# The bonus and the output gate of a delta-rule scan formed in the projections' stage instead of per unit of the scan

## The chip, the cores and the metric

The kernel runs on one core of a Trainium2 chip. A core has a matrix engine (TensorE, in the profile PE, its weight loads PEld), a vector engine (VectorE, DVE), a scalar engine (ScalarE, ACT), a general one (GpSimd, POOL) and a queue from which DMA transfers are issued (SyncE, SP). The metric is the time of one execution on the device in microseconds, less being better; the time of a kernel is the median of three runs.

## The reference

Two layers over 1024 tokens of width 1024, all in float32. The first has a convolution and a gated unit as its mixer, the second RWKV-7 time mixing; each is followed by a feed-forward block. The change touches the time mixing alone, whose last lines matter here:

```python
w_log = -softplus(-(w0 + tanh(xw @ w_w1) @ w_w2)) - 0.5      # low-rank map, inner width 64
a = sigmoid(a0 + (xa @ a_w1) @ a_w2)                         # low-rank map, inner width 64
g = sigmoid(xg @ g_w1) @ g_w2                                # the gate, inner width 128
...
# per token: state <- state * w + (state . -kk) (kk * a)^T + v k^T ;  y = state . r
y = groupnorm(y) * ln_g + ln_b
bonus = sum(r * k * r_k, over the 64 channels of a head) * v
y = y + bonus
return (y * g) @ w_out
```

There are 16 heads of 64 channels. `r`, `k` and `v` are products of a shifted mixture of the tokens with three 1024x1024 matrices.

## The kernel before

**Stages.** In order: the convolution mixer, the first feed-forward block, the projections (`phase_c`), the scan (`phase_d`), the output projection of the time mixing (`phase_e`), the second feed-forward block.

**Precision.** Products of large matrices are made of three (`mm3`, `proj_T`, `proj_tok`): weights and activations are split into a high and a low part, and high x high, low x high and high x low are summed. `load_unit` loads a piece of 128x1024 weights and splits it, the high part on ScalarE (`whi`), the low one on VectorE (`wlo`). The scan's small products are in float32 or float16.

**Projections.** `phase_c` goes through two halves of 512 tokens: `do_r(0)`, `do_k(0)`, `do_v(0)`, `do_k(1)`, `do_r(1)`, `do_v(1)`. Between their large products, light jobs are woven in by `step`: the two low-rank maps (`light` and `lora2`, with tiles `pl`; the inner width of 64 is stored as 64 high and 64 low columns, `whl`), the inner half of the gate (`ghid`), and the mixing of tokens. The results `r`, `k`, the normalised `k` and so on go to DRAM tensors (`scr_R`, `scr_K`, ..., `scr_v`), one transfer per 128x512 block, issued from SP's queue.

**Scan.** The recurrence is done by chunks of 64 tokens, 16 chunks and two groups of eight heads: 32 units. A unit is a set of generators, each of which does one step when it is called: `load` and `load_v` fetch its data; `cumulate` (E) and `decay` (D) form the running decays; `scores` (P) forms the products within the chunk (`pA`), masks them (`ra`, the lower triangle copied to `lt`), the bonus (`pb`), the keys' transposes (`ptm`) and the triangle's transposes (`pL`); `inverse` (I) inverts the triangle in five doublings of two steps (`pX`, `pQ`, with copies by ScalarE and VectorE); `chain` (C) makes the products with the state: `pz`, its copy `zr`, `p`, `py`, `pS`, the normalisation (`gve`, `grs`) and the gate (`pg`, copied to `gg`); `store` (Y) writes the result.

**Order.** One iteration of the scan's loop advances unit i in C, unit i+1 in I, unit i+2 in P and later ones in D and E. The string `ORDER` says in which order their steps are emitted. Only the first matmul of a step is fixed against its neighbours (`keep` with `pace`); the framework's scheduler may move the rest within an engine's queue. After each step of C, I or P the loop yields; the first 32 such turns (`SCAN_EARLY`) run inside `do_v(1)`, between its products `pv`, the others inside `phase_e`, which weaves the loads of its own weights (`w_o`) and the first pieces of its work between them.

**The pieces in question.** Per unit, the bonus takes on POOL a product of `r` and `k`, on TensorE eight products of one column (`pb`), on VectorE a copy (`bon`). The gate takes two products of 64x256 (`pg<-g,ghid`) in float32 from `ghid`, which stays in SBUF, and a copy by ScalarE.

Of the kernel before, what the change touches and what calls it, by code (L numbers as in the profile page):

```python
# [25 lines left out]
P = 128  # L26
# [32 lines left out]
def f(ap):  # L59
    return ap.bitcast(F32)  # L60
# [16 lines left out]
ORDER = "ICIPCEIPDICPIECDICPIYCICPDICI"  # L77
# [12 lines left out]
def build(tc, xT, xtok, w_ab, w_abv, w_abo, cols, rows, hrows, sguw, f_in, f_out, w_r, w_k, w_v, w_o,  # L90
          l_w1, l_a1, l_g1, l_w2, l_a2, l_g2, out, dbg=None):
    nc = tc.nc
    c = Ctx()
    c.tc, c.nc = tc, nc
    c.first_loads = None
    with ExitStack() as es:
        setup(c, es, rows, hrows)
        dram = es.enter_context(tc.tile_pool(name="dram", bufs=1, space=DRAM))
        xres = dram.tile([T, D], F32, name="xres")
        scr = {n: dram.tile([8, P, 8, P], F32, name=f"scr_{n}") for n in ("R", "K", "KN", "KA", "SW")}  # L100
        scrv = dram.tile([T, D], F32, name="scr_v")
        scry = dram.tile([T, D], F32, name="scr_y")

        def show(n, tiles):
# [11 lines left out]
        scan = phase_d(c, scr, scrv, scry, l_g2)  # L116
        phase_c(c, x1, scr, scrv, w_r, w_k, w_v, l_w1, l_a1, l_g1, l_w2, l_a2, scan)
# [711 lines left out]
def phase_c(c, x1, scr, scrv, w_r, w_k, w_v, l_w1, l_a1, l_g1, l_w2, l_a2, scan):  # L829
    nc = c.nc  # L830
    sel2 = c.scan.sel2
    ghid = c.ghid = big(c, "ghid")
# [49 lines left out]
    def light(h, i, src, m, func, out):  # L882
# [6 lines left out]
        def steps():  # L889
# [25 lines left out]
            if not pair:  # L915
                nc.scalar.activation(out, p, func)
                return
# [8 lines left out]
            split(c, out[0][0:m], out[1], t_)  # L926
            if pair:
                nc.vector.tensor_copy(out[0][m:], f(out[0][0:m]))
# [10 lines left out]
    def lora2(u, hid, k):  # L939
        p = bank(c, "c", "pl")  # L940
        s = slice(k * P, (k + 1) * P)
        nc.tensor.matmul(p, u[:, s], hid[0], start=True, stop=False)
        c.last_mm = nc.tensor.matmul(p, u[0:64, s], hid[1], start=False, stop=True)
        return p

    def low_rank(h):

        hid = []
        for n in range(2):
            t_ = c.pool.tile([P, 1024], F32R, name="hid", tag="row", bufs=2)  # L950
            hid.append((t_[:, 0:512], t_[0:64, 512:1024]))
# [15 lines left out]
    def gate(h):  # L967
        light(h, 5, l_g1, P, AF.Sigmoid, ghid[:, h * TH:(h + 1) * TH])
# [79 lines left out]

    sp = Ring(c, "sp", 512, 4)
# [9 lines left out]
    xk = heavy(1, 2)  # L1059
    do_v(0, xv, rest)  # L1060
# [18 lines left out]
def scan_const(c):  # L1079
# [8 lines left out]
                            channel_multiplier=-1)  # L1088
    s.ident16 = const.tile([P, P], F16, name="ident16")
# [58 lines left out]
def phase_d(c, scr, scrv, scry, l_g2):  # L1148
# [19 lines left out]
    ghid, R1 = c.ghid, {}  # L1168
# [9 lines left out]
    rings([("R", 3), ("cl", 2), ("Em", 2), ("rk", 2), ("S", 2 * NG), ("dS", 2), ("u1", 2), ("y", 3),  # L1178
           ("V", 4), ("gg", 2), ("bo", 2)], W)
# [11 lines left out]
    for b in R1["G"].bufs + R1["lt"].bufs + [f(b) for b in R1["TT"].bufs]:  # L1191
        nc.gpsimd.memset(b, 0.0)
    S = [None] * NG
# [34 lines left out]
    def load_v(u):  # L1228

        src = scrv[u.ch * CH:(u.ch + 1) * CH, u.g * 2 * W:(u.g + 1) * 2 * W].rearrange(  # L1230
            "t (k e j) -> t e k j", k=HP, e=2)
        u.UV = R1["UV"]().rearrange("p (e k j) -> p e k j", e=2, k=HP)
        u.V = A4(R1["V"]())
        for e in range(2):
            nc.sync.dma_start(u.UV[half[e], e], src[:, e])
            nc.sync.dma_start(u.V[half[e]], src[:, e])
# [21 lines left out]
    def decay(u):  # L1258
# [6 lines left out]
        u.bk, u.rk = A4(R1["bk"]()), A4(R1["rk"]())  # L1265
# [6 lines left out]
        for e in range(2):  # L1272
            nc.gpsimd.tensor_tensor(u.rk[half[e]], ld["R"][half[e]], u.xk[half[e], :, e, :], op=ALU.mult)
        yield

    def scores(u):
# [31 lines left out]
        yield  # L1308
# [6 lines left out]
        nc.vector.copy_predicated(level_view(u.Tm, 1, False), sc.mT[1].unsqueeze(3), level_view(u.L, 1, False))  # L1315
# [33 lines left out]
    def chain(u, nxt):  # L1349
# [73 lines left out]
        nc.gpsimd.tensor_tensor(bo, u.V, bc(u.bon), op=ALU.mult)  # L1423
        nc.gpsimd.tensor_tensor(y, y, bo, op=ALU.add)
        yield
        pg = A4(bank(c, "c", "pg")[:, 0:W])
        for e in range(2):
# [35 lines left out]
    for i in range(-INV - 1, len(seq)):  # L1463
# [15 lines left out]
        if i > 0:  # L1479
            gens["Y"] = store(us[i - 1])  # L1480
        if i == 0:
            g2 = c.pool.tile([P, 1024], F32, name="g2", tag="w", bufs=N_W)
            nc.sync.dma_start(g2, l_g2)
            g2 = g2.rearrange("p (g k e j) -> p g e k j", g=NG, k=HP, e=2)
# [185 lines left out]
```

## Time and profile before

| | us |
|---|---|
| median of three runs | 2592.91 (2592.89 to 2593.0) |
| the profiled execution, its time | 2591.67 |
| its span, first to last instruction | 2590.0 |
| projections up to the last value projection, 1026.0 to 1343.0 | 317.0 |
| last value projection with the scan's first turns, 1343.0 to 1397.0 | 54.0 |
| scan, units 4 to 10 | 97.2 |
| scan, units 11 to 27 | 208.3 |

The profile was taken of one execution. "Busy" is the time in which an engine works on an instruction; x is a number of instructions; PEclk is the share of full speed that TensorE's clock was granted, with two levels, 1.2 and 2.4 GHz. A row of the timeline has the start in us, the duration in us, the engine, the line of the kernel, the operation, what is written and read, the shape, and in brackets the time that the engine sat idle before and what ended it. Units of the scan are counted from 0, from one `gve` to the next.

### The profile page before, as it was taken

What the parts mean: (1) busy time and instruction counts of PE and PEld (TensorE: products, weight loads), DVE (VectorE), ACT (ScalarE), POOL (GpSimd) and SP (SyncE); (2) the same over time, 40 slices, a digit from 0 to 9 for tenths busy, and PEclk for the clock granted to TensorE, in tenths of its full rate; (3) what the DMA queues carried; (4) which work ended last, traced back from release to release, by engine and by line L of the source; (5) the groups of instructions that cost most, each with busy time, mean ns of one, the idle gap of its engine ahead of it and who ended that gap; (6) DMA issues with size and microseconds to landing.
All of it is one profiled execution on the core that took longest, in us unless ns stands there. A gap on an engine that the chain in (4) does not pass through costs nothing.

```text
span 2590.0 us, 41379 instructions
## 1 busy us (share of the span) xinstructions
PE 2487.4 (96%) x16064; PEld 1981.5 (77%) x16064; DVE 1703.2 (66%) x2981; ACT 1135.7 (44%) x2192; POOL 519.0 (20%) x526
## 2 busy tenths in 40 slices
PE   8999989999999999999999888889999999999997
PEld 6677867888878787677777777777877888878785
DVE  7766596665657545878775778875676666657444
ACT  3115553333322334868655767774452233232230
POOL 0011250000006000010112666666300000006004
PEclk9999999999999999999999989999999999999998
DMA  4403222222225452555575444423412222225441
GB/s 149 128 9 122 90 98 96 83 74 85 85 95 195 140 177 90 155 143 174 166 195 142 101 102 105 88 59 101 155 66 98 82 82 81 82 101 197 156 157 65
DMA packets 257605, 295.79 MB, mean 114 GB/s; under 512 B 149888, under 2 KB 190976, under 8 KB 257408
## 3 DMA queue, kind: packets, MB, share of 16 engines
q1 hardware_dynamic: 256256, 291.05, 36.2%
q8 instruction: 126, 2.06, 0.3%
q10 hardware_dynamic: 1152, 2.10, 0.2%
q14 instruction: 71, 0.58, 0.1%
HBM read 219.56 MB, written 69.21 MB: 111 GB/s over the span
## 4 chain that ended last, share of the span: by engine, by line
PE 68%; DVE 10%; issue 9%; ACT 5%; DMA 5%; POOL 3%; SPq 0%; DVEq 0%; ACTq 0%; POOLq 0%
PE py L646 14%; PE pz L646 9%; PE px L646 8%; PE po L232 2%; DMA wraw<-in_f_out_dram 2%; PE po L233 2%; PE po L234 2%; PE pd L232 2%; PE pd L233 2%; PE pd L234 2%; PE pv L232 2%; PE pX L1204 1%; PE pv L233 1%; PE pA L1204 1%; PE pv L234 1%
## 5 line engine op out<-in xcount | busy, mean ns | idle before, releaser
L646 PE MATMUL py<-xch,wb 128*128 128x512 f32 x1056 | 355.7, 399 | 3.2 <-DVE u L695 2.8
L200 ACT CAST wb<-wraw 128x512 fp32r<-128x512 f32 x220 | 135.6, 620 | 394.3 <-PE py L646 177.9
L232 PE MATMUL pd<-wb,hh 128*128 128x512 f32 x704 | 277.1, 394 | 3.4 <-DVE acc L735 3.3
L234 PE MATMUL pd<-wb,hl 128*128 128x512 f32 x704 | 277.2, 394 | 0.0
L233 PE MATMUL pd<-wb,hh 128*128 128x512 f32 x704 | 276.8, 393 | 0.0
L646 PEld LDWEIGHTS py<-xch,wb 128*128 128x128 f32 x1056 | 199.6, 189 | 61.9 <-DVE u L695 16.0
L355 POOL TENSOR_TENSOR acc<-acc,g_row 128x1024 f32<-128x1024 f32 x24 | 67.4, 2807 | 889.9 <-DMA acc<-res 882.4
L203 DVE TENSOR_TENSOR wb<-wraw,wb 128x512 fp32r<-128x512 f32 x220 | 171.4, 783 | 103.6 <-ACT wb L200 101.2
L646 PE MATMUL px<-xch,wb 128*128 128x512 f32 x704 | 234.5, 396 | 3.2 <-ACT p L657 3.2
L646 PE MATMUL pz<-xch,wb 128*128 128x512 f32 x704 | 233.0, 392 | 4.5 <-ACT xch L200 4.5
L200 ACT CAST wb<-sums 128x512 fp32r<-128x512 f32 x176 | 108.9, 621 | 257.5 <-PE pz L646 144.6
L646 PE MATMUL py<-xcl,wb 128*128 128x512 f32 x528 | 208.6, 395 | 1.1 <-DVE xcl L203 0.9
L203 DVE TENSOR_TENSOR wb<-sums,wb 128x512 fp32r<-128x512 f32 x176 | 123.2, 703 | 107.0 <-ACT wb L200 106.1
L203 DVE TENSOR_TENSOR hl<-wraw,hh 128x1024 fp32r<-128x1024 f32 x72 | 124.2, 1734 | 87.8 <-ACT hh L200 87.7
L232 PEld LDWEIGHTS pd<-wb,hh 128*128 128x128 f32 x704 | 132.7, 189 | 35.5 <-DVE acc L735 4.5
L646 PEld LDWEIGHTS px<-xch,wb 128*128 128x128 f32 x704 | 132.9, 189 | 35.0 <-ACT p L657 4.7
L646 PEld LDWEIGHTS pz<-xch,wb 128*128 128x128 f32 x704 | 132.2, 188 | 34.4 <-ACT xch L200 5.3
L233 PEld LDWEIGHTS pd<-wb,hh 128*128 128x128 f32 x704 | 132.4, 188 | 29.6
L234 PEld LDWEIGHTS pd<-wb,hl 128*128 128x128 f32 x704 | 132.3, 188 | 29.4
L193 DVE TENSOR_TENSOR wlo<-wraw,whi 128x1024 fp32r<-128x1024 f32 x82 | 105.1, 1289 | 60.0 <-ACT whi L192 36.3
L1204 PEld LDWEIGHTS <-lt 128*128 128x128 f16 x1792 | 84.1, 99 | 73.9 <-issue 49.1
L646 PE MATMUL px<-xcl,wb 128*128 128x512 f32 x352 | 139.5, 396 | 0.0
(313 smaller groups left out, 5615.1 us busy)
## 6 DMA issues: line engine op xcount, KB each, us to landing
wraw<-in_f_in_dram SPq DMA_DIRECT2D x96, 512.0 KB, 3.6
wraw<-scr_h SPq DMA_DIRECT2D x72, 512.0 KB, 3.6
scr_h<-hf SPq DMA_DIRECT2D x44, 512.0 KB, 2.6
wraw<-in_f_out_dram SPq DMA_DIRECT2D x88, 256.0 KB, 2.8
res<-acc SPq DMA_DIRECT2D x16, 512.0 KB, 2.6
acc<-res SPq DMA_DIRECT2D x16, 512.0 KB, 4.2
wraw<-in_w_r_dram SPq DMA_DIRECT2D x16, 512.0 KB, 4.1
wraw<-in_w_k_dram SPq DMA_DIRECT2D x16, 512.0 KB, 4.2
```

The source lines that it names most:

```text
L193: (lo_eng or nc.vector).tensor_tensor(lo, raw, f(hi), op=ALU.subtract)
L200: nc.scalar.copy(hi, src)
L203: return (eng or nc.vector).tensor_tensor(lo, src, f(hi), op=ALU.subtract)
L232: nc.tensor.matmul(ps, ls(ah), rs(bh), start=start, stop=False)
L233: nc.tensor.matmul(ps, ls(ah), rs(bl), start=False, stop=False)
L234: c.last_mm = nc.tensor.matmul(ps, ls(al), rs(bh), start=False, stop=stop)
L355: c.nc.gpsimd.tensor_tensor(x, x, rows[0], op=ALU.mult)
L646: c.last_mm = nc.tensor.matmul(ps, a_[:, k * P:(k + 1) * P], b_[:, k % 2, :], start=start and k == i == 0, stop=False, skip_group_check=True)
L1204: keep(nc.tensor.matmul(*a, **k))
```

## The change

The gate is formed in `phase_c`: `ghid` is split into a high and a low part, and `gates(h)` makes for each half of the tokens eight tiles of 128x512 by three products each, copies them and stores them to a DRAM tensor `scr_g`. The bonus's sums are formed there too: `bonus(h)` loads the blocks of `r` and `k` back, multiplies them on POOL and sums over channels by products with `rkb`, a matrix of 128x2 that holds `r_k` for the two heads of a block (`pbn`), and stores them to `scr_b`. In the scan, a unit loads its gate (two transfers more, 15 instead of 13 per unit) and finds the sums in `bon`. The products `pb` and `pg`, POOL's product and two copies are gone from the unit. `scores` makes the triangle's transposes as its third step and the keys' as its fourth; before it was the keys' in its fourth and the triangle's in its fifth. The low-rank products with the low half use full 128x128 weights, where one operand was 64 columns (L903) or 64 rows (L943) before.

```diff
-ORDER = "ICIPCEIPDICPIECDICPIYCICPDICI"
+ORDER = "ICIPCEIPDICCIECDIPIYCIPDICI"
...
-                    nc.tensor.matmul(p[0:m, :], u[:, k, 0, :], r[k // 2][1][:, k % 2, 0:TH],
+                    nc.tensor.matmul(p, u[:, k].rearrange("p e m -> p (e m)"), r[k // 2][1][:, k % 2, 0:TH],
...
-        c.last_mm = nc.tensor.matmul(p, u[0:64, s], hid[1], start=False, stop=True)
+        c.last_mm = nc.tensor.matmul(p, u[:, s], hid[1], start=False, stop=True)
...
+    def gates(h):
+        g2 = load_unit(c, l_g2)
+        for t in range(4 * h, 4 * h + 4):
+            for n in range(2):
+                p = bank(c, "b", "pg")
+                mm3(c, p, ghid, g2, True, True, lambda g: g[:, t * P:(t + 1) * P], lambda w: w[:, n * 512:(n + 1) * 512])
+                gg = tmp(c, "gg")
+                nc.scalar.copy(gg, p)
+                nc.sync.dma_start(scrg[t * P:(t + 1) * P, n * 512:(n + 1) * 512], gg)
+                if (t, n) != (4 * h + 3, 1):
+                    yield
...
+    def bonus(h):
+        out = c.pool.tile([P, 4, 2, 8], F32, name="bons", tag="bons", bufs=1)
+        rk = None
+        for k in range(KT + 1):
+            if k:
+                p = bank(c, "b", "pbn", [P, 4, 2])
+                for t in range(4):
+                    nc.tensor.matmul(p[:, t, :], rk[:, t * P:(t + 1) * P], c.scan.rkb[:, k - 1, :], start=True, stop=True)
+                nc.vector.tensor_copy(out[:, :, :, k - 1], p)
+            if k < KT:
+                pair = []
+                for n in "RK":
+                    t_ = tmp(c, "rk")
+                    nc.sync.dma_start(t_.rearrange("p (c t) -> p c t", c=4),
+                                      scr[n][4 * h:4 * h + 4, :, k, :].rearrange("c p t -> p c t"))
+                    pair.append(t_)
+                rk = pair[0]
+                nc.gpsimd.tensor_tensor(rk, rk, pair[1], op=ALU.mult)
+                yield
...
+    add(gates(0), KT)
+    add(bonus(0), KT + 1)
     do_v(0, xv, rest)
...
+    add(gates(1), KT)
     do_r(1, xr, rest)
 
+    add(bonus(1), KT + 1)
     turns = itertools.islice(scan, SCAN_EARLY)
     do_v(1, xv, turn=lambda k: k % 2 and next(turns, None))
...
+            nc.sync.dma_start(u.gg[half[e]], src[1][:, e])
...
-        pb = bank(c, "c", "pb")
-        for k, e in PAIRS:
-            mm(pb[half[e], k:k + 1], u.rk[half[e], k, :], c.colr("r_k", u.g * HP + k, 1)[half[e]],
-               start=True, stop=True)
-        u.bon = small(c, [P, HP], "bon", "bon", NA)
-        nc.vector.tensor_copy(u.bon, pb[:, 0:HP])
-        yield
...
-        pg = A4(bank(c, "c", "pg")[:, 0:W])
-        for e in range(2):
-            mm(pg[half[e]], ghid[:, ch * CH:(ch + 1) * CH], g2[:, g, e], start=True, stop=True)
-        gg = A4(R1["gg"]())
-        nc.scalar.copy(gg, pg)
-        nc.gpsimd.tensor_tensor(y, y, gg, op=ALU.mult)
+        nc.gpsimd.tensor_tensor(y, y, u.gg, op=ALU.mult)
```

The scan's program moves at three places. The first is TensorE's queue in the last value projection, where `pv` are the value products and `pX`, `pQ` belong to the inverse of the first unit. Before:

```order
L234 MATMUL pv<-whi,xil 128x512
L1204 LDWEIGHTS lt
L1204 MATMUL pX<-lt 128x64
...
L1204 LDWEIGHTS lt
L1204 MATMUL pQ<-lt 128x64
...
L232 MATMUL pv<-whi,xih 128x512
L233 MATMUL pv<-wlo,xih 128x512
L234 MATMUL pv<-whi,xil 128x512
L232 MATMUL pv<-whi,xih 128x512
L233 MATMUL pv<-wlo,xih 128x512
L234 MATMUL pv<-whi,xil 128x512
L1204 MATMUL pA<-ra 128x128 x4
```

The same place now, with `pbn` the bonus's products:

```order
L236 MATMUL pv<-whi,xil 128x512
L1070 MATMUL pbn<-rkb,rk 128x2 x4
L1252 LDWEIGHTS lt
L1252 MATMUL pX<-lt 128x64
...
L1252 LDWEIGHTS lt
L1252 MATMUL pQ<-lt 128x64
...
L1070 MATMUL pbn<-rkb,rk 128x2 x4
...
L1255 MATMUL pL<-ident_3074,lt 128x128
...
L1070 MATMUL pbn<-rkb,rk 128x2 x4
...
L234 MATMUL pv<-whi,xih 128x512
L235 MATMUL pv<-wlo,xih 128x512
L236 MATMUL pv<-whi,xil 128x512
```

Before, six value products stand between any two steps of the first inverse; now ten such steps, with one set of the triangle's transposes and four groups of the bonus's products, stand without a value product between them.

The second place is TensorE's queue in a unit in the middle of the scan, at the first products of the chain (`pz`) and the scores of the next unit but one (`pA`). Before, in every unit:

```order
L1204 MATMUL pz<-R,ra 64x64 x8
L1204 MATMUL pz<-ra 64x64 x8
L1204 LDWEIGHTS lt
L1204 MATMUL pX<-lt 128x64
...
L1204 LDWEIGHTS lt
L1204 MATMUL pQ<-lt 128x64
...
L1204 MATMUL pA<-ra 128x128 x4
L1204 MATMUL p_15286<-zr,TT 128x64 x4
L1204 LDWEIGHTS lt
L1204 MATMUL pX<-lt 128x64
...
L1204 MATMUL pA<-ra 128x128 x4
```

Now, in units 11 to 27 (units 1 to 10 keep the arrangement above):

```order
L1252 MATMUL pz<-R,ra 64x64 x8
L1252 LDWEIGHTS lt
L1252 MATMUL pQ<-lt 128x64
...
L1252 MATMUL pA<-ra 128x128 x3
L1252 MATMUL pz<-ra 64x64
L1252 MATMUL pA<-ra 128x128 x3
L1252 MATMUL pz<-ra 64x64 x7
L1252 LDWEIGHTS lt
L1252 MATMUL pX<-lt 128x64
...
L1252 MATMUL p_16491<-zr,TT 128x64 x4
...
L1252 MATMUL pA<-ra 128x128 x2
```

Six of the eight score products now stand among the products of `pz`, ahead of the product that reads their copy.

The third place is ScalarE's queue in the same unit, at the copy `zr` of `pz`. Before:

```order
L1413 ACTIVATE gve<-mv 128x4
L1345 CAST TT<-pX 32x4x32
L1328 CAST lt<-pX 128x128x2
L1306 COPY lt<-ident_3067 128x512
L1369 CAST zr<-pz 128x256
L1307 COPY lt<-ident_3067 128x512
L1375 COPY R<-p_15040 128x256
L1328 CAST lt<-pX 128x64x4
L1288 CAST lt<-ra 64x4x64
```

Now (L1335 is the copy of the triangle out of the masked scores, L1408 that of `pz`):

```order
L1367 CAST lt<-pX 128x128x2
L1339 COPY lt<-ident_3074 128x512
L1340 COPY lt<-ident_3074 128x512
L1452 ACTIVATE gve<-mv 128x4
L1335 CAST lt<-ra 64x4x64
L1408 CAST zr<-pz 128x256
L1414 COPY R<-p_15099 128x256
```

The first of a unit's two copies of the triangle stood behind `zr` and stands ahead of it now. Elsewhere, the loads of the output projection's weights, which stood in units 4, 5 and 7, stand in units 23 to 25.

## Rows read from the trace of the kernel before

**Rows 1.** The page: span, and busy time of each engine.

```profile
span 2590.0 us, 41379 instructions
PE 2487.4 (96%) x16064; PEld 1981.5 (77%) x16064; DVE 1703.2 (66%) x2981; ACT 1135.7 (44%) x2192; POOL 519.0 (20%) x526
```

**Rows 2.** Busy time by stage: projections, last value projection, units 4-10, 11-27.

```profile
core 0: us, PE busy (x) PEld busy (x) DVE busy (x) ACT busy (x) POOL busy (x), PEclk, DMA share, GB/s
1026.00:1343.00 317.00, 309.33 (x1510) 230.19 (x1509) 247.23 (x374) 235.61 (x386) 32.24 (x20) 0.99 0.57 167
1343.00:1397.00 54.00, 53.28 (x385) 39.35 (x386) 24.64 (x51) 23.55 (x57) 5.78 (x8) 1.00 0.63 170
1452.90:1550.10 97.20, 83.90 (x1425) 72.53 (x1422) 75.59 (x206) 66.70 (x193) 60.36 (x72) 0.86 0.43 100
1550.10:1758.40 208.30, 181.33 (x3475) 155.08 (x3472) 161.01 (x479) 152.25 (x444) 127.49 (x168) 1.00 0.37 80
```

**Rows 3.** The same view of single units of the scan: 4, 10 and 17.

```profile
1452.90:1468.20 15.30, 13.19 (x213) 11.49 (x210) 11.26 (x30) 10.26 (x30) 8.63 (x10) 0.78 0.44 108
1535.10:1550.10 15.00, 13.18 (x182) 11.47 (x184) 11.73 (x31) 9.21 (x27) 9.42 (x11) 0.66 0.32 71
1624.00:1636.50 12.50, 10.82 (x214) 9.21 (x210) 9.98 (x29) 9.12 (x29) 7.68 (x10) 1.00 0.40 87
```

**Rows 4.** Chain of waits, end of a unit: start us, us on it, what.

```profile
1621.79 0.34 PE pL L1207 x4
...
1622.15 0.58 ACT lt L1313
...
1623.06 0.41 PE pX L1204 x8
1623.47 0.37 ACT R L1430
```

**Rows 5.** Timeline of TensorE in the projections, low-rank maps and norms.

```profile
1078.51 0.39 PE L901 MATMUL pl<-xih,whl 128*128 128x512 f32 x1
1078.73 0.40 PE L903 MATMUL pl<-xil,whl 128*64 128x512 f32 x1
1078.97 0.39 PE L901 MATMUL pl<-xih,whl 128*128 128x512 f32 x1
...
1113.86 0.40 PE L942 MATMUL pl<-hid,whl 128*128 128x512 f32 x1
1114.19 0.50 PE L943 MATMUL pl<-hid,whl 64*128 64x512 f32 x1
1114.62 0.50 PE L232 MATMUL pk<-xih,whi 128*128 128x512 f32 x1
...
1115.28 0.63 PE L989 MATMUL pn<-sel,k 128*64 128x2 f32 x16
1115.84 0.50 PE L234 MATMUL pk<-xih,wlo 128*128 128x512 f32 x1
```

**Rows 6.** One tile's instructions, min/median/max ns: weight loads of fp32 transposes.

```profile
L1010 PEld LDWEIGHTS pb<-ident,rx x64: 137/140/143, 1133.6 to 1299.9; 128*128 128x128 f32 x64
```

**Rows 7.** Timeline of unit 17: the pieces removed, and the scores' copies.

```profile
1625.27 0.71 PE L1204 MATMUL pA<-ra 64*128 64x128 f32 x8
...
1627.36 1.34 DVE L1286 COPY_PREDICATED ra<-mA,pA 128x512 f32<-128x512 uint8 x2 [1.26 <-PE pA L1204]
1627.61 0.68 PE L1204 MATMUL pz<-R,ra 64*64 64x64 f32 x16
1628.13 0.40 ACT L1288 CAST lt<-ra 64x256 f16<-64x256 f32 x1 [0.89 <-DVE ra L1286]
1628.15 0.63 PE L1204 MATMUL pb<-colt,R 64*64 64x1 f32 x16
...
1629.92 1.25 SPq L1236 DMA_DIRECT2D R<-scr_v  x2
...
1634.63 0.65 PE L1204 MATMUL pg<-g,ghid 128*64 128x256 f32 x4
```

**Rows 8.** Low parts of the output projection's weights on VectorE, min/median/max ns.

```profile
L193 DVE TENSOR_TENSOR wlo<-wraw,whi x4: 1611/1616/1627, 1456.1 to 1794.8; 128x1024 fp32r<-128x1024 f32 x4
```

More of the change, by code (lines that the diff above doesn't have):

```diff
@@ L115, in build @@
             nc.sync.dma_start(dbg["b"], xres)
-        scan = phase_d(c, scr, scrv, scry, l_g2)
-        phase_c(c, x1, scr, scrv, w_r, w_k, w_v, l_w1, l_a1, l_g1, l_w2, l_a2, scan)
+        scan = phase_d(c, scr, scrv, scry, scrb, scrg)
+        phase_c(c, x1, scr, scrv, scrb, scrg, w_r, w_k, w_v, l_w1, l_a1, l_g1, l_w2, l_a2, l_g2, scan)
         if dbg is not None and "R" in dbg:
@@ L824, in ffn, with phase_c @@
     return dest
-def phase_c(c, x1, scr, scrv, w_r, w_k, w_v, l_w1, l_a1, l_g1, l_w2, l_a2, scan):
+def phase_c(c, x1, scr, scrv, scrb, scrg, w_r, w_k, w_v, l_w1, l_a1, l_g1, l_w2, l_a2, l_g2, scan):
     nc = c.nc
     sel2 = c.scan.sel2
-    ghid = c.ghid = big(c, "ghid")
+    ghid = [big(c, f"ghid{i}", F32R) for i in range(2)]
     def spill(n, k, h, src):
@@ L925, in steps @@
                 nc.scalar.activation(t_, p[0:m, :], func)
-            split(c, out[0][0:m], out[1], t_)
+            split(c, out[0][0:m], out[1][0:m], t_)
             if pair:
-                nc.vector.tensor_copy(out[0][m:], f(out[0][0:m]))
+                for a in out:
+                    nc.vector.tensor_copy(a[m:], f(a[0:m]))
         add(steps(), KT + 1)
@@ L967, in gate @@
     def gate(h):
-        light(h, 5, l_g1, P, AF.Sigmoid, ghid[:, h * TH:(h + 1) * TH])
+        light(h, 5, l_g1, P, AF.Sigmoid, [g[:, h * TH:(h + 1) * TH] for g in ghid])
+    def gates(h):
[9 more added lines that the diff above has]
+                    yield
     def do_k(h, ha, xi):
@@ L1047, in do_v @@
                 step(7 - n * 4 - t)
+    def bonus(h):
[17 more added lines that the diff above has]
+                yield
+        for t in range(4):
+            for i in range(2):
+                nc.sync.dma_start(scrb[h * 8 + t * 2 + i].rearrange("e t k -> t e k"), out[i * CH:(i + 1) * CH, t])
     sp = Ring(c, "sp", 512, 4)
@@ L1088, in scan_const @@
                             channel_multiplier=-1)
+    s.rkb = const.tile([P, 8, 2], F32, name="rkb")
+    nc.vector.memset(s.rkb, 0.0)
+    for e in range(2):
+        nc.vector.tensor_copy(s.rkb[e * 64:e * 64 + 64, :, e], c.colr("r_k", 0, 8)[e * 64:e * 64 + 64, :])
+    s.bon = const.tile([P, T // CH, 8], F32, name="bon")
     s.ident16 = const.tile([P, P], F16, name="ident16")
@@ L1192, in phase_d @@
         nc.gpsimd.memset(b, 0.0)
+    bon = sc.bon
     S = [None] * NG
@@ L1228, in load_v @@
     def load_v(u):
-        src = scrv[u.ch * CH:(u.ch + 1) * CH, u.g * 2 * W:(u.g + 1) * 2 * W].rearrange(
-            "t (k e j) -> t e k j", k=HP, e=2)
+        src = [a[u.ch * CH:(u.ch + 1) * CH, u.g * 2 * W:(u.g + 1) * 2 * W].rearrange(
+            "t (k e j) -> t e k j", k=HP, e=2) for a in (scrv, scrg)]
         u.UV = R1["UV"]().rearrange("p (e k j) -> p e k j", e=2, k=HP)
-        u.V = A4(R1["V"]())
+        u.V, u.gg = A4(R1["V"]()), A4(R1["gg"]())
         for e in range(2):
-            nc.sync.dma_start(u.UV[half[e], e], src[:, e])
-            nc.sync.dma_start(u.V[half[e]], src[:, e])
+            nc.sync.dma_start(u.UV[half[e], e], src[0][:, e])
+            nc.sync.dma_start(u.V[half[e]], src[0][:, e])
+            nc.sync.dma_start(u.gg[half[e]], src[1][:, e])
     def cumulate(u):
@@ L1289, in scores @@
         yield
-        pb = bank(c, "c", "pb")
-        for k, e in PAIRS:
-            mm(pb[half[e], k:k + 1], u.rk[half[e], k, :], c.colr("r_k", u.g * HP + k, 1)[half[e]],
-               start=True, stop=True)
-        u.bon = small(c, [P, HP], "bon", "bon", NA)
-        nc.vector.tensor_copy(u.bon, pb[:, 0:HP])
-        yield
-        p = bank(c, "c", "ptm", [P, HP, P])
-        for k in range(HP):
-            tr(p[:, k, :], u.bk[:, k, :], c.ident)
-        u.bktm = A4(R1["bktm"]())
-        nc.scalar.copy(u.bktm, p)
         u.Tm, u.Tt = A4(R1["Tm"]()), A4(R1["Tt"]())
@@ L1315, in scores @@
         nc.vector.copy_predicated(level_view(u.Tm, 1, False), sc.mT[1].unsqueeze(3), level_view(u.L, 1, False))
+        yield
+        p = bank(c, "c", "ptm", [P, HP, P])
+        for k in range(HP):
+            tr(p[:, k, :], u.bk[:, k, :], c.ident)
+        u.bktm = A4(R1["bktm"]())
+        nc.scalar.copy(u.bktm, p)
         yield
@@ L1422, in chain @@
         bo = A4(R1["bo"]())
-        nc.gpsimd.tensor_tensor(bo, u.V, bc(u.bon), op=ALU.mult)
+        nc.gpsimd.tensor_tensor(bo, u.V, bc(bon[:, ch, g * HP:(g + 1) * HP]), op=ALU.mult)
         nc.gpsimd.tensor_tensor(y, y, bo, op=ALU.add)
-        yield
-        pg = A4(bank(c, "c", "pg")[:, 0:W])
-        for e in range(2):
-            mm(pg[half[e]], ghid[:, ch * CH:(ch + 1) * CH], g2[:, g, e], start=True, stop=True)
-        gg = A4(R1["gg"]())
-        nc.scalar.copy(gg, pg)
-        nc.gpsimd.tensor_tensor(y, y, gg, op=ALU.mult)
+        nc.gpsimd.tensor_tensor(y, y, u.gg, op=ALU.mult)
         u.y = y
@@ L1480, in phase_d @@
             gens["Y"] = store(us[i - 1])
+        if i in (0, NG * 4):
+            h = slice(0, 8) if i == 0 else slice(8, 16)
+            nc.sync.dma_start(bon[:, h, :], scrb[h].rearrange("c e t k -> (e t) c k"))
         if i == 0:
-            g2 = c.pool.tile([P, 1024], F32, name="g2", tag="w", bufs=N_W)
-            nc.sync.dma_start(g2, l_g2)
-            g2 = g2.rearrange("p (g k e j) -> p g e k j", g=NG, k=HP, e=2)
             lg, lb = by_half("rln_g"), by_half("rln_b")
```

19 lines of the change are left out of this document (8 added, 11 removed).

## The prediction

> **What bounds the kernel now.** I read the busy times of the engines first: TensorE is busy for 2487.4 of the 2590.0 us [rows 1], so an instruction added to TensorE, or taken from it, counts unless its stage waits for something else. Second, the windows by stage. In the projections TensorE is busy for 309.3 of 317.0 us, in the last value projection, where the scan begins, for 53.3 of 54.0: there work on TensorE is paid at its full price. In the scan it is busy for 181.3 of 208.3 us only, with VectorE at 161.0 and ScalarE at 152.3 [rows 2]. One unit of the scan (a chunk of 64 tokens and half of the heads) takes 12.4 us (17 units lie in those 208.3, the last of them shorter): a ring of short steps between TensorE, ScalarE and VectorE. So there I read, third, the chain of waits of one unit. Near its end stand the triangle's transposes (0.34), their copy by ScalarE (0.58) and, between the last product of the inverse and the copies that follow from it, the gate's copy (0.37) [rows 4]. The bonus's small products are not on it.
>
> **What the change costs and saves.** The profiled execution took 2591.67 us, 1.24 below the median of 2592.91. The sum is made against 2591.67, and 1.24 is added at the end.
>
> A, gates on TensorE: 48 products of 128x512 (16 tiles, three products each) come into a stage that TensorE fills. Such a product follows the one before after 0.22 us, the next after 0.24 [rows 5]. 48 x 0.23 = **+11.0**. ScalarE (235.6 of 317.0 busy) has room for their 16 copies [rows 2]. The 16 stores, like the bonus's 16 stores and 32 loads, lie on SP's queue in a stage whose DMA engines are busy for 0.57 [rows 2]; I cost them at nothing there.
>
> B, bonus on TensorE: 64 products with 128x128 fp32 weights and two columns. None like it is in the trace. The nearest row is the weight load of that shape, 0.140 us [rows 6]: 64 x 0.14 = **+9.0**. Below: the norms' sums, also two columns but half the weights, took 0.56 for 16 [rows 5], twice that for one whole stationary is 0.07, so +4.5. Above: a full product each, +14.7. I take the weight load, since with two columns little else is left. POOL's 16 products more lie on an engine busy for 32 of 317 us [rows 2].
>
> C, full low-rank maps: 32 products whose weights had 64 rows get 128. The start of the 64-row product came 0.33 us after the one before it, and the next start 0.43 after that [rows 5]; at 0.23 for each, 0.10 + 0.20 is saved: 32 x 0.293 = **-9.4**; if those gaps had another cause, 0. The 32 products that get 128 columns where they had 64 cost nothing: such a one already holds TensorE for the same 0.24 [rows 5].
>
> The Trainium skill, "TensorE: Matmul & The Clock Gate", Why this matters for your kernels, says that one product with K=32 takes as long as one with K=128; by it C would be zero and the sum 9.4 higher. The row differs from it: the starts are 0.33 and 0.43 apart here, not 0.23.
>
> D, the last value projection: before, six value products stand between two steps of the first inverse (and cover its copies); in the changed order ten steps of it stand in a row, with only four groups of the bonus's products between. Each step then shows its copy. By the chain two such copies keep TensorE from 1622.13 to 1623.06 [rows 4], about half a microsecond each, with the short products 0.6: ten make **+6**. Between 0 (the products displaced fill later gaps) and +12 (VectorE's queue doubles each).
>
> E, the units of the scan with a clean order. Taken out of each unit: the bonus's 16 issues of TensorE (0.63) and the gate's (0.65) [rows 7], 1.28 in all; on the chain of waits the triangle's transposes, their copy and the gate's copy, 0.34 + 0.58 + 0.37 = 1.29 [rows 4]. The transposes stay, but three steps earlier, where the next unit's inverse does not wait for them. I take 1.25 per unit (the two readings overlap; at least 0.4, when the keys' copy takes the triangle's place; at most 1.9). By the order, units 1 to 10 keep the arrangement of before: 10 x 1.25 = **-12.5**. SP's queue issues 15 transfers per unit where it issued 13, at 0.62 each [rows 7]: 9.3 us, hidden under 11. Units 11 to 27 follow; the few at the ends I leave at nothing.
>
> F, the loads of the output projection's weights. Before, they stand in units 4 to 7, and units 4 to 10 took 97.2 us [rows 2], 10.4 above seven of 12.4. In the changed order they stand in units 23 to 25. The one fall of the clock in a unit without such a load (15.0 us at 0.66 [rows 3]) cost 2.6; the other 7.8 goes with the loads (their low parts are 1.61 each on VectorE [rows 8]) and is paid again later: **-2.6**.
>
> G, units 11 to 27 have another order on TensorE: the products of the next unit's scores stand among the first products of the chain of the state, and on ScalarE the copy of a score's triangle stands ahead of the chain's copy `zr`. So `zr` waits for six products (0.53 at 0.71 for eight), one copy on VectorE (half of 1.34) and the triangle's copy (0.40) [rows 7]: 1.6 us, where it stood right behind its own product. The 14 that hold no load: 12.4 - 1.25 + 1.6 = 12.75 each, 14 x 0.35 = **+4.9**. Bounds: nothing late, -17.5; a microsecond more in each, +14.
>
> H, the clock. Units with a granted clock below 1 take longer: 15.3 us at 0.78, 15.0 at 0.66, against 12.5 [rows 3], so a fall to the lower level (1.2 in place of 2.4 GHz) for part of a unit costs 2.6. Of the seven units of 1452.9 to 1550.1, where TensorE worked 83.9 of 97.2 us, four had one (mean 0.86); the 17 after it had none [rows 2]. The late units now make TensorE wait longer for its neighbours, as those did. I take three falls more: **+7.8**, from none to one in every second unit (+18).
>
> Sum: 11.0 + 9.0 - 9.4 + 6 - 12.5 - 2.6 + 4.9 + 7.8 = +14.2, so 2605.9, and with 1.24 **2607 us** as a median. Its own range is 2599 to 2612.
>
> **Rivals.**
> 1. Slower still: the late units behave like units 4 to 10 and the clock falls in every second one: 18.2 in place of 7.8, so 2618; in all of them 2636. For it: four falls in seven units before. Against it: 17 quiet ones behind them. Chance 0.10.
> 2. Faster: the copies ahead of `zr` end before its own product does, so that nothing in G waits. TensorE reaches the scores early enough where it stood idle for 1.7 of 12.5 us [rows 3]. Then G is -17.5 and H nothing: 14.2 - 22.4 - 7.8 = -16.0, that is 2577. It decides whether the triangle's copy ends before the last of the 16 products into `pz`, 0.68 us after their start [rows 7]. Against it: VectorE's queue holds other copies ahead of it, and it is busy for 10 of 12.5 us [rows 3]. With B at its lower bound 2572. Chance 0.25.
> 3. No change: the late units lose what they gain (12.4 each) and the clock does not fall: 14.2 - 4.9 - 7.8 = +1.5, that is 2594; if half of 1.6 is hidden, 2588. Chance 0.18.
> 4. Narrow outputs cost too, not narrow weights alone: then the 32 products of C that get 128 columns save 9.4 more, and the time is 2598. The rows speak against it: the products of 128*64 and 128*128 follow each other at 0.22 and 0.24 [rows 5]. Chance 0.04. The Trainium skill, "TensorEngine Tiling (Array Packing)", Key Properties, would have it so: it says that a change of the tiling mode drains TensorE. The trace agrees for 64 rows, not for 64 columns.
>
> **How the numbers follow.** A repeated measurement of this kernel can tell about 0.2% (5 us) from no change. The forecast has 0.43, the rivals 0.10, 0.25, 0.18 and 0.04. Faster: rival 2 and the edge of rival 3, 0.27. Same: the rest of rival 3 and rival 4, 0.20. Slower: 0.53. The range from 2575 to 2622 leaves out the lower part of rival 2 (0.11) and the upper of rival 1 (0.07).
>
> **What would show it.** A and B: the projections' stage longer by some 20 us before C, with TensorE still above 97% busy, and starts 0.14 apart in the bonus's groups. C: products of the low-rank maps at 0.23 from start to start. D: waits of TensorE for ScalarE and VectorE in the last value projection, 54 us before. E: units 1 to 10 at 11.2 us, with no gate's copy on the chain of waits. G: units 11 to 27 at 12.7, `zr` starting more than a microsecond after the end of `pz`. H: granted clocks below 1 in late units. I would be wrong above all if G's copies ended in time (rival 2), or if the bonus's loads held up the last weights of the values, which stand behind them on SP's queue: then D is larger than its bound.

## The result and the profile after

2667.5 us against 2593.0: the changed kernel takes 1.0288 times as long (95% interval 1.0276 to 1.0301), 75 us more; forecast were 14. The profiled execution took 2665.82 us. The page, as in [rows 1]:

```profile
span 2664.1 us, 40588 instructions
PE 2543.2 (95%) x15600; PEld 2047.4 (77%) x15600; DVE 1709.8 (64%) x2976; ACT 1138.4 (43%) x2180; POOL 486.0 (18%) x478
```

The windows of the stages, with the columns of [rows 2]: projections, last value projection, units 0 to 9, units 10 to 29:

```profile
1026.00:1355.80 329.80, 318.25 (x1590) 249.74 (x1589) 244.64 (x373) 239.62 (x381) 41.90 (x26) 0.97 0.62 182
1355.80:1448.40 92.60, 78.96 (x544) 62.91 (x543) 39.73 (x88) 36.69 (x94) 11.67 (x10) 0.85 0.64 165
1448.40:1560.80 112.40, 92.36 (x1817) 80.69 (x1817) 94.74 (x272) 86.61 (x253) 59.13 (x78) 0.97 0.48 103
1560.80:1865.80 305.00, 273.53 (x3703) 234.95 (x3705) 190.44 (x551) 176.13 (x508) 130.86 (x166) 0.75 0.39 91
```

TensorE runs fewer instructions and is busy for 56 us more. Its granted clock was between 0.86 and 1.00 in the stages of [rows 2]; now it is 0.75 in the last of the four. The stages between marks that both traces have (last product of r, each `gve`), in us, beside the sum of the prediction by its terms:

| stretch | before | after | difference | forecast |
|---|---|---|---|---|
| up to the last product of r | 1338.3 | 1355.5 | +17.2 | A + B/2 + C = +6.1 |
| from there to unit 0 | 66.0 | 92.9 | +26.9 | B/2 + D = +10.5 |
| units 0 to 10 | 145.8 | 124.9 | -20.9 | E - 10.4 = -22.9 |
| units 11 to 27 | 208.3 | 259.5 | +51.2 | 7.8 + G + H = +20.5 |
| after them | 831.6 | 831.3 | -0.3 | 0 |

The units, as in [rows 3]: one of the early ones (unit 8), a late one at full clock (20), a late one as most are (17), and one of the two longest (24), which holds a load of weights:

```profile
1538.90:1549.70 10.80, 8.98 (x187) 7.86 (x184) 9.12 (x27) 8.78 (x27) 6.26 (x8) 1.00 0.47 102
1706.40:1719.30 12.90, 10.51 (x185) 8.85 (x184) 9.21 (x28) 8.73 (x27) 5.72 (x8) 1.00 0.31 66
1661.00:1676.60 15.60, 14.36 (x185) 12.53 (x184) 9.21 (x28) 8.77 (x27) 5.72 (x8) 0.67 0.38 82
1766.40:1784.80 18.40, 17.34 (x188) 14.96 (x187) 10.19 (x29) 9.73 (x28) 5.71 (x8) 0.50 0.32 70
```

The early unit shows E, the late one at full clock G (12.9, forecast 12.75); the others are the clock. Of units 11 to 27, 15 had a granted clock below 1, where three falls were forecast. The timeline of unit 17 (15.6 us) has the copies of G:

```profile
1662.22 0.73 DVE L1333 COPY_PREDICATED ra<-mA,pA 128x512 f32<-128x512 uint8 x1 [1.84 <-PE pA L1252]
...
1662.99 0.41 ACT L1335 CAST lt<-ra 64x256 f16<-64x256 f32 x1 [1.76 <-DVE ra L1333]
1663.30 0.36 ACT L1408 CAST zr<-pz 128x256 fp32r<-128x256 f32 x1
...
1663.71 0.87 PE L1252 MATMUL p<-zr,TT 128*128 128x64 f32 x4 [0.70 <-ACT zr L1408]
```

The windows of that unit have the fall behind them:

```profile
1661.00:1664.00 3.00, 2.30 (x30) 1.93 (x29) 1.50 (x3) 0.90 (x4) 2.46 (x4) 0.99 0.33 73
1664.00:1674.20 10.20, 10.20 (x125) 9.10 (x125) 5.50 (x14) 5.57 (x17) 3.25 (x5) 0.50 0.39 85
1674.20:1676.60 2.40, 1.85 (x36) 1.50 (x34) 2.21 (x11) 2.30 (x7) 0.00 (x0) 1.00 0.38 85
```

`zr` stands behind the masked scores and the triangle's copy, TensorE waits 0.7 us for it, and from there the clock is at 1.2 GHz for 10 us. In the last value projection TensorE waits longest for the bonus, then for the second weights of the values; SP's queue (SPq) issued both late:

```profile
1393.07 0.40 PE L1252 MATMUL pQ<-lt 128*128 128x64 f16 x4
1399.72 1.87 PE L1070 MATMUL pbn<-rkb,rk 128*128 128x2 f32 x8 [6.25 <-POOL rk L1080]
...
1408.57 0.80 PE L234 MATMUL pv<-whi,xih 128*128 128x512 f32 x1 [2.27 <-ACT whi L194]
...
1394.29 0.38 SPq L1076 DMA_DIRECT2D rk<-scr_R  x1
1398.98 1.13 SPq L179 DMA_DIRECT2D wraw<-in_w_v_dram  x2
...
1358.05 0.81 SPq L979 DMA_DIRECT2D scr_g<-gg  x2
1358.95 0.46 SPq L1267 DMA_DIRECT2D ld<-scr_SW  x1
```

TensorE's waits of this stage, and its clock behind them (the column before the last two):

```profile
PE pbn L1070 <- POOL rk L1080: 6.2, 1, 6.2
PE pX L1252 <- ACT lt L1367: 2.9, 5, 0.8
PE pv L234 <- ACT whi L194: 2.3, 1, 2.3
PE pX L1252 <- DVE lt L1376: 1.7, 3, 0.9
PE pv L235 <- DVE wlo L195: 0.5, 1, 0.5
...
1391.00:1418.20 27.20, 15.63 (x96) 12.45 (x94) 10.58 (x27) 9.29 (x25) 4.54 (x4) 0.50 0.67 176
```

(A row of waits has who waited for whom, the us in total, the times, the longest.) Ahead of the load at 1394.29, SP's queue issued the 13 loads of one unit and a store. The last pair of rows of the timeline shows one source of the crowd: the scan's first load follows the last gate store at once, at 1359, while before the change it started at 1307. Gate tiles, the bonus's `rk` and the scan's loads take turns in one ring of eight.

### The profile page after: what moved, and what is told of

It is laid out like the page before. It is cut to its first block, busy times and chain, and to the rows that moved or that the text cites. A ratio compares the mean times of both kernels' runs of the same rounds, so it can differ in the third digit from the quotient of the medians.

```text
span 2664.1 us, 40588 instructions
## 1 busy us (share of the span) xinstructions
PE 2543.2 (95%) x15600; PEld 2047.4 (77%) x15600; DVE 1709.8 (64%) x2976; ACT 1138.4 (43%) x2180; POOL 486.0 (18%) x478
## 5 line engine op out<-in xcount | busy, mean ns | idle before, releaser
L1252 PEld LDWEIGHTS <-lt 128*128 128x128 f16 x1792 | 94.5, 109 | 72.8 <-issue 42.1
```

The costliest lines, as they stand in the source:

```text
L1252: keep(nc.tensor.matmul(*a, **k))
```

## The experiments

**Pinned order.** `keep` holds every matmul of the scan behind the one before it, not the first of a step alone.

```diff
-        if fresh[0]:
-            pace(c, ins)
-        fresh[0] = False
+        pace(c, ins)
```

> The changed kernel with every matmul of the scan held in the order in which it is written, so that units 11 to 27 have on TensorE the order of units 1 to 10; nothing else differs. Theory (the scrambled order makes the late units slow, and the clock falls because of the waits it makes): units 11 to 27 take 11 to 11.6 us instead of 14.5 to 18, no fall of the clock in most of them, and the time is 2605 to 2615 us. Rival (the late units are slow because less work per unit leaves TensorE idle, or because of the 64 loads of the gate): they stay at 14 us and more, and the time stays above 2650.

2637.8 us (ratio 1.0163, 1.015 to 1.0176): 30 us less than the changed kernel. Windows of an early and a late unit:

```profile
1545.00:1556.20 11.20, 9.13 (x189) 8.01 (x186) 8.98 (x28) 8.68 (x28) 6.24 (x8) 1.00 0.47 102
1644.50:1657.50 13.00, 10.48 (x187) 9.33 (x186) 9.65 (x28) 8.66 (x27) 6.24 (x8) 0.87 0.45 99
```

VectorE's timeline in the late one:

```profile
1646.99 1.34 DVE L1331 COPY_PREDICATED ra<-mA,pA 128x512 f32<-128x512 uint8 x2 [1.70 <-PE pA L1250]
1648.23 1.22 DVE L1289 TENSOR_TENSOR_SCAN R<-rst,ld 128x256 f32<-128x256 f32 x1
1649.37 0.41 DVE L1374 CAST_PREDICATED lt<-mk,pX 128x256 f16<-128x256 uint8 x1
```

Neither theory's number: most late units take 12.7 to 13.0. Units 11 to 27 together take 220.0 us, in the changed kernel 259.5, so that the order on TensorE is worth 2.3 us per unit, the clock included. On VectorE the running decay's scan stands ahead of a copy of the inverse in the late unit, and TensorE waits up to 1.6 us for that copy, in the early unit up to 0.8.

**Bonus early.** One block per step of the projection of r.

```diff
+            if more and k:
+                next(more)
...
-    do_r(1, xr, rest)
-
-    add(bonus(1), KT + 1)
+    late = bonus(1)
+    do_r(1, xr, rest, late)
+
+    add(late, 2)
```

> The changed kernel with the bonus of the second half of the tokens woven into the preceding projection: each block is loaded one step after it is stored, so its products end before the scan's loads begin. Theory (in the last value projection TensorE waits for bonus loads that stand behind some 14 loads of a scan unit on SP's queue, then for weights behind those, and the clock falls): the time from the last product of r to unit 0's normalisation goes from 93 us to 66 to 70, the late units run in the clean order at 11 to 11.6 us, and the time is 2575 to 2585. Rival (the transfers of the gate, or the smaller number of turns per unit, hold that stage): it stays above 80 us and the time above 2600.

2663.9 (1.0261, 1.0247 to 1.0275). Missed: the last product of r came 13 us later, at 1369, the stage behind it took 84 us, with a wait of 6.5 for the weights of the values, and units from 16 on had the scrambled order again.

**No second bonus.** The kernel leaves out the second half's sums; the scan reads the first half's in their place.

```diff
-    add(bonus(1), KT + 1)
...
-            nc.sync.dma_start(bon[:, h, :], scrb[h].rearrange("c e t k -> (e t) c k"))
+            nc.sync.dma_start(bon[:, h, :], scrb[0:8].rearrange("c e t k -> (e t) c k"))
```

> The changed kernel without the second half's bonus: its loads, products and stores are left out and the first half's sums are used for it. Theory: like the kernel with the bonus woven in early, less 32 products of 0.24 us, that is 7.5 us lower: 2567 to 2578. Rival (the wait comes from the scan's own loads): the last value projection stays above 80 us and the time above 2595.

2637.4 (1.0162, 1.0144 to 1.0179). Missed: the stage took 77.6, still with 4.6 of waiting for weights. The second half's bonus is 15 of the 27 us by which this stage had grown, not all of them.

**Full rows alone.** The kernel before with term C.

```diff
-                    nc.tensor.matmul(p[0:m, :], u[:, k, 0, :], r[k // 2][1][:, k % 2, 0:TH],
+                    nc.tensor.matmul(p, u[:, k].rearrange("p e m -> p (e m)"), r[k // 2][1][:, k % 2, 0:TH],
...
-        c.last_mm = nc.tensor.matmul(p, u[0:64, s], hid[1], start=False, stop=True)
+        c.last_mm = nc.tensor.matmul(p, u[:, s], hid[1], start=False, stop=True)
```

> The kernel before with the low-rank products on full weights and nothing else of the change. By the gaps in the trace of before (0.33 and 0.43 us between starts where 0.23 is usual, 32 products) it is faster by 9.4 us, that is 2583 to 2584. Rival (the gaps have another cause, a product with 64 rows takes no longer than one with 128): no change, 2592 to 2594.

2586.5 (0.9967, 0.9955 to 0.9978), 9 us faster, as forecast. The products stand at 0.24 us and less from start to start, where [rows 5] had 0.33 and 0.43:

```profile
1110.94 0.40 PE L234 MATMUL pl<-xih,wlo 128*128 128x512 f32 x1
1111.18 0.40 PE L943 MATMUL pl<-hid,whl 128*128 128x512 f32 x1
1111.42 0.40 PE L944 MATMUL pl<-hid,whl 128*128 128x512 f32 x1
1111.65 0.40 PE L232 MATMUL pk<-xih,whi 128*128 128x512 f32 x1
```

**Gate loads on ScalarE's queue.**

```diff
-            nc.sync.dma_start(u.gg[half[e]], src[1][:, e])
+            nc.scalar.dma_start(u.gg[half[e]], src[1][:, e])
```

> The changed kernel with the scan's two gate loads per unit issued from ScalarE's queue instead of SP's, nothing else. Theory (the two transfers more on SP's queue make a unit's other loads late; by that the order on TensorE and VectorE changes from unit 11 on, and the clock falls with the waits): units 11 to 27 take 11 to 11.8 us, as units 1 to 10 do, the last value projection stays at 90 to 98 us, and the time is 2598 to 2612. Rival (the loss in the late units is the loads' own, on whatever queue, or the order on VectorE that also the pinned kernel has): late units of 13 us and more, time above 2630.

2730.7 (1.0525, 1.0509 to 1.054). The theory missed, and the time lies where the rival had it, but by neither reason: nearly all units, early ones too, take 15 to 16. TensorE's order was clean in every one of them. ScalarE's waits in 100 us with six units, and one of them in the timeline:

```profile
ACT lt L1335 <- issue: 27.1, 6, 4.5
...
1606.22 0.72 POOL L1464 TENSOR_TENSOR R<-R 128x256 f32<-128x256 f32 x1
1606.98 1.53 ACTq L1285 DMA_DIRECT2D R<-scr_g  x2
1608.55 0.83 ACT L1335 CAST lt<-ra 64x256 f16<-64x256 f32 x2 [4.52 <-issue]
```

ScalarE stands still for 4.5 us per unit ahead of the triangle's copy: its last instruction before ended at 1604.03, 1.5 us go to the two issues, and in each of the six units these start within 0.04 us of the end of POOL's product with an earlier unit's gate (L1464). The loads wait for that product to release a gate tile, so far as the times tell, and ScalarE's copies wait behind them. As a test of the order this run is spoilt by that.

**Gate tiles apart.**

```diff
-                gg = tmp(c, "gg")
+                gg = sp()
```

> The changed kernel with the gates' staging tiles taken from the ring of four that the other stores use, not from the ring of eight that the scan's first loads need too; nothing else. Theory (the scan's first loads wait until the last gate tile is stored, at 1358 us instead of 1307, so its steps and the value weights come late and TensorE waits in the last value projection): the first such load starts before 1320 us, the stage from the last product of r to unit 0 goes from 93 to 72 to 80 us, the late units stay at 15, and the time is 2645 to 2657. Rival (the bonus's loads on SP's queue make that wait): the stage stays above 88 us, the time above 2660.

2674.5 (1.0306, 1.0285 to 1.0327). Missed: the scan's first load moved from 1359 to 1333, the stage from 93 to 83 us; but in the projections TensorE now waited 5.3 us for ScalarE's copy of a gate, and they ended 12 us later. Unit 0 comes at 1450.5, no earlier than in the changed kernel: to free that ring of the gate tiles alone does not bring it forward.

**Both.** The two edits before this together.

> Both edits together (gate tiles from the stores' ring, gate loads on ScalarE's queue), the bonus still formed beside the last value projection. If the two causes are independent and account for the loss, the stage takes 72 to 80 us, every unit 11 to 11.8, and the time is 2578 to 2592, faster than before. Rival (one of the two hides the other, or a third cause is left): above 2600.

2731.7 (1.053, 1.0514 to 1.0546): ScalarE's issues spoil it as above. Unit 0 comes at 1451.3.

**Gate moved, bonus kept.** As the run before it, with `pb` back as third step of the scores and no bonus ahead of the scan.

> As the kernel with both edits, but with the bonus's products back in the scan (third step of the scores) and the bonus's stage taken out; gates moved, triangle's transposes ahead, full rows kept. Theory: the gates cost 11.0 and the full rows give 9 in the projections, the last value projection takes 65 to 68 us, and the units lose the 1.25 us of the gate's copy and the triangle's transposes on the chain of waits, the bonus's 0.63 on TensorE lying beside it: 2560 to 2575. Rival (what makes the units shorter is the bonus's products leaving TensorE): units of 12 us and more, 2580 to 2595.

2694.7 (1.0389, 1.0372 to 1.0407), units of 16 us for the same reason. Ahead of the scan it tells much: the last product of r is at 1340.2 and the stage behind it takes 68.1 us, without a wait above 0.8. Unit 0 comes at 1408.3, in the changed kernel at 1448.4 and in the run before this one, which has gate tiles and gate loads as here, at 1451.3: the bonus ahead of the scan, with the waits and falls that it brings, costs 40 us and more. That is shared by both halves: the last product of r comes at 1340.2 here, at 1355.5 in the changed kernel, and at 1357.2 where the bonus's tiles were taken out of the ring, too (all repaired, below).

**Thirteen transfers.** Values and gates stored in a unit's order; the value's copy and the gate come in one transfer each.

```diff
...
-            nc.sync.dma_start(u.V[half[e]], src[0][:, e])
-            nc.sync.dma_start(u.gg[half[e]], src[1][:, e])
+        nc.sync.dma_start(V, src[0])
+        nc.sync.dma_start(gg, src[1])
```

> The changed kernel with the values and the gates stored in the order in which a unit reads them (ScalarE's copy puts them so), by which the value's second copy and the gate come in one transfer each instead of two: 13 transfers per unit on SP's queue as before the change, the same bytes, nothing else. Theory (the two transfers more per unit on SP's queue moved the order on TensorE and VectorE in the late units, and ScalarE's queue was no remedy since ScalarE has to wait there for each issue): all units 11.0 to 11.9 us, few falls of the clock, the last value projection still 90 to 97 us: 2598 to 2613. Rival (the order on VectorE or the smaller work per unit makes the clock fall anyway): late units of 12.8 us and more, above 2630.

2687.4 (1.0367, 1.0351 to 1.0383). The theory of the number of transfers falls: the order on TensorE was clean, and units took up to 21 us. Waits of VectorE (1550 to 1750 us) and of SP's queue (1560 to 1760):

```profile
DVE R L1293 <- DMA ld<-scr_SW: 46.8, 13, 6.2
...
SPq L1287 <- POOL R L1466: 46.7, 13, 8.1
```

SP's queue stops at the gate's load until POOL has ended its product with an earlier gate (L1466) and so released a tile; the decays queued behind come late, and VectorE waits for them. It is the wait at the head of the queue that costs the time here, not the number of transfers.

The same with the bonus kept, and with both moved and the gate tiles apart:

> The kernel with the gate moved and the bonus kept in the scan, gate tiles from the stores' ring, now with all loads on SP's queue, 13 transfers per unit by the merged loads. Theory: projections and last value projection as in the run with the bonus kept (unit 0 at about 1408 us), every unit 11.2 to 12.0: 2555 to 2572, faster than before by 1%. Rival (without the bonus's products leaving TensorE a unit stays at 12.4): 2580 to 2592.

> Gate and bonus moved, gate tiles from the stores' ring, 13 transfers per unit. Against the run before it in this list this tells what the bonus's move is worth by itself. Theory: units 11.0 to 11.6, about 0.4 shorter than with the bonus kept (27 units, 10 us), and 64 products of 0.24 (15 us) and the waits of the last value projection (10 to 18 us) against it: 2572 to 2592, slower than with the bonus kept. Rival (the bonus's work in the scan costs more than it does ahead): faster than with the bonus kept.

2698.2 (1.0408, 1.0392 to 1.0424) and 2697.3 (1.0404, 1.039 to 1.0419): the same wait, 44.3 us in 12 units and 43.4 in 10.

**The decay's scan held, too.** On top of the pinned kernel, with the step E, which emits that scan, later in `ORDER`:

```diff
-ORDER = "ICIPCEIPDICCIECDIPIYCIPDICI"
+ORDER = "ICIPCIPDICCICDIPIYCEIPDICEI"
...
+        if c.ysub:
+            after(c, run, c.ysub)
...
+        c.ysub = nc.vector.tensor_tensor(y, py, bc(mv[:, :, 0]), op=ALU.subtract)
```

> As the pinned kernel (every matmul of the scan in the order of the text), and on VectorE the running-decay scan of a later unit held behind the subtraction of the mean of `py`, where the early units of the changed kernel often have it, not ahead of the copies of the inverse. Theory (what is left of 13.0 us against 11.2 in the late units of the pinned kernel is that scan of 1.2 us in front of a copy that TensorE waits for, and the short fall of the clock that follows): late units 11.0 to 11.9, 2612 to 2622. Rival (the fall of the clock comes from the smaller work per unit): they stay at 12.5 and more, above 2630.

2630.4 (1.0146, 1.0132 to 1.016). The late units without a load take 11.5, or 12.2 to 12.7 where the clock falls for 3 us, about as the theory has it; a window of such a unit at full clock:

```profile
1657.60:1669.10 11.50, 9.02 (x187) 7.85 (x184) 9.55 (x29) 8.82 (x27) 6.18 (x8) 1.00 0.46 99
```

From unit 0 to the last `gve` are 379 us, in the changed kernel 426, before 397. Units 11 to 27 take 208.2 us, in the changed kernel 259.5. The time is 8 us above its range and just inside the rival's, mostly because unit 0 came 7 us later, at 1455; three of the late units took 12.5 to 12.7, which is the rival's number.

**All repaired.** As the run before this, with gate tiles apart, the bonus's `rk` out of the ring, and the second half's bonus during units 2 to 10.

```diff
-                gg = tmp(c, "gg")
+                gg = sp()
...
+                t2 = big(c, "rk")
...
-    add(bonus(1), KT + 1)
+    c.late = bonus(1)
...
+        if 2 <= i < 3 + KT:
+            next(c.late, None)
```

> The same, with the gate tiles taken from the stores' ring and the second half's bonus formed during units 2 to 10 of the scan, one block per unit, in place of the last value projection. Theory: the scan's steps and the value products alternate again, so unit 0 ends at 1405 to 1418 us, as before the change, units take 11.0 to 11.9 (0.3 to 0.9 more in the nine with a block of the bonus), and the time is 2565 to 2582, faster than before. Rival (the loads on SP's queue hold VectorE's scan in the units, as in the runs with 13 transfers): units of 15 us and more, above 2640.

2650.7 (1.0218, 1.0204 to 1.0232). Missed: the last value projection is mended (70.9 us), but four units took 21 to 23: their bonus products stood on TensorE ahead of their data.

```profile
PE pbn L1071 <- POOL rk L1082: 28.5, 4, 7.3
```

**Bonus loaded two units ahead.**

```diff
-        for k in range(KT + 1):
-            if k:
...
+        for k in range(KT + lag):
+            if k >= lag:
```

> As the run before it (everything pinned, gate tiles apart, second half's bonus during the scan), with each block's loads now two units ahead of its products and POOL's product one unit ahead, so that TensorE no longer meets a product whose data are on the way. Theory: the four units of 21 to 23 us become 12, the time is 2600 to 2612, and what is left over the kernel before lies ahead of unit 0 (20 us later). Rival (the 256 KB loads hold SP's queue for the scan's own loads): units 2 to 11 stay at 14 us and more, above 2630.

2621.1 (1.0113, 1.0093 to 1.0132), 9 us above its range: one unit of 21 us is left (a wait of 6.9), and unit 0 at 1430.8.

**Gate moved, all pinned.** Bonus in the scan, 15 transfers on SP's queue, gate tiles apart, TensorE's order and VectorE's scan held, four tiles in place of three for the scan's `r`.

```diff
-ORDER = "ICIPCEIPDICCIECDIPIYCIPDICI"
+ORDER = "ICIPCIPDICPICDICPIYCEIPDICEI"
...
-    rings([("R", 3), ("cl", 2), ("Em", 2), ("S", 2 * NG), ("dS", 2), ("u1", 2), ("y", 3),
+    rings([("R", 4), ("cl", 2), ("Em", 2), ("rk", 2), ("S", 2 * NG), ("dS", 2), ("u1", 2), ("y", 3),
...
```

> Gate moved, bonus kept in the scan, TensorE's order and VectorE's scan pinned, gate tiles from the stores' ring, 15 transfers per unit on SP's queue, and one more tile for the scan's copy of r, so that its load needn't wait for POOL's product of the bonus. Theory: unit 0 at 1405 to 1412 us, units 11.5 to 12.3: 2565 to 2585, faster than before. Rival (VectorE's scan waits for its load, which stands on SP's queue behind transfers that wait for POOL, as in the run with 13 transfers and the bonus kept): units of 15 us and more, above 2650.

2581.8 (0.9959, 0.9946 to 0.9972), within its range and faster than the kernel before by 0.4%, of which the full rows alone are 0.33% (0.9955 to 0.9978): the intervals overlap, so that no gain of the moved gate is shown. Unit 0 comes at 1411.5; units as this one:

```profile
1447.40:1459.00 11.60, 10.01 (x205) 8.89 (x202) 10.73 (x30) 8.79 (x28) 7.46 (x10) 1.00 0.50 109
```

## Why the prediction was wrong

The sign and most mechanisms were right; 60 of the 75 us were not in the sum (11 in the projections, 16 in the last value projection, 31 in units 11 to 27, 2 in units 0 to 10).

- **H** is the step that failed most: "I take three falls more". A fall's price was right (15.6 against 12.9 us: 2.7, forecast 2.6), their number was not: 15 of 17 late units. At 12.75 each and with 7.8 for loads those units would be 225 us; they took 259.5, so H was about 35 us instead of 7.8. Its bound, a fall in every second unit, was too low as well, though four falls in the seven disturbed units of before [rows 2] spoke for more.
- **G** was right: 12.9 at full clock, though only unit 20 shows it here (units 19 and 20 of the run with gate tiles apart took 12.9, too). The pinned runs show the order's part: some 15 us in most late units became 13.0, and 11.5 to 12.7 with VectorE's scan held too, and the clock fell for shorter times. The place of that scan was not in the prediction.
- **D** was undersized. TensorE's waits in the stage are 13.6 us (6.2 + 2.9 + 2.3 + 1.7 + 0.5 in the view of waits), against 6 and a bound of 12, and the clock at 0.50 for 27 us behind them was not in it. "Each step then shows its copy" was the smaller part (4.6); the larger (9.0) were the bonus's loads and the weights, named only as what would make the prediction wrong. The ring that holds the scan's first loads until 1359 was overlooked.
- **The projections' stage** had no term for waits or the clock. A and C as measured and half of B (7.2) make 9.2 of its 17.2 us. TensorE's waits there are 11.2 us, before 7.5, and the clock was at 0.50 behind two of them, one of 2.3 us for the mixed tokens (to 1199.2) and one of 0.5 for the bonus's `rk` (to 1253.3):

```profile
1202.00:1206.00 4.00, 4.00 (x11) 3.13 (x10) 2.63 (x4) 3.50 (x5) 0.00 (x0) 0.50 0.50 155
1256.00:1260.00 4.00, 4.00 (x24) 3.31 (x25) 4.00 (x7) 4.00 (x8) 1.47 (x1) 0.50 0.10 6
```

- **B** took its upper bound: the timeline of TensorE around one group has 1.36 us from the product of k ahead of it to the second one behind, where two such intervals are 0.46; that is 0.225 for each of the four, 14.4 for 64. The lower bound misread its row: the source has eight of the norms' products where the row has 16 instructions, so that twice the price of one is 0.14, not 0.07.

```profile
1241.62 0.39 PE L234 MATMUL pk<-xih,whi 128*128 128x512 f32 x1
1241.85 0.95 PE L1070 MATMUL pbn<-rkb,rk 128*128 128x2 f32 x8
1242.66 0.48 PE L235 MATMUL pk<-xil,whi 128*128 128x512 f32 x1
1242.98 0.39 PE L236 MATMUL pk<-xih,wlo 128*128 128x512 f32 x1
```

- **A** held: from the first product of r to the last are 313.9 us with the bonus kept and 302.9 with full rows alone, 11.0 for the gates. **C** held: 9.0 measured, 9.4 forecast (9.6 by its own 0.10 + 0.20); rival 4 would have made it twice that. The Trainium skill, "TensorE: Matmul & The Clock Gate", Why this matters for your kernels, says that one product with K=32 takes as long as one with K=128. Here, where products of 64 rows stood between products of 128, full rows for 32 of them gave 9.0 us.
- **E**, and F's part in the early units, held: 20.9 for units 0 to 10, forecast 22.9; units 1 to 9 take 11.3 on average, forecast 11.15. In the late units less of it is left even with the order held: 12.0 on average in units 11 to 22, where the scan is held too, against 12.4 before.

What is not settled: why the clock falls in these units. TensorE's waits in a late unit (7.6 + 7.1 us in 11 units) are no longer than in an early one (14.1 + 4.7 in ten), but placed otherwise; no run varies that place alone. Why the framework's scheduler scrambles the units from 11 on is not shown by a trace either; that the order, not the work, costs the time in units 11 to 27 is shown by the two pinned runs, which do the same work in 220.0 and 208.2 us instead of 259.5. Why the clock falls behind a wait in the projections is open as well.

## What to carry to other kernels

Work that is moved into a full stage is paid there at full price, and the waits that it brings to its new neighbours can cost more than itself: here unit 0 came 40 us later for 15 us of products. When a change lets a scheduler reorder, read the order in late iterations, on every engine, and pin what the chain of waits depends on before timing the idea. Where a change shifts TensorE's waits, count the shift in every iteration that has it, and with it the clock, which fell in 15 of 17 late units here and not in three.

## What the runs showed of the hardware

- A transfer issued from ScalarE's queue can stop ScalarE's own work: 4.5 us per unit with two loads of 64 KB, some 3.0 of them until POOL's product with an earlier gate had ended, 1.5 for the issues. On SP's queue the same loads waited 0.2 us in 200.
- An fp32 product of two columns with 128x128 weights takes 0.225 us, as long as one of the large products with 512 columns (0.23). The trace has eight instructions for a group of four such products, two for each, and as many weight loads, where the 64 transposes of [rows 6] have 64.
